# Six query and key pairs by seven half-size products, and partial sums kept in PSUM

## The chip, the cores and the metric

The kernel runs on one core of one Trainium2 chip. The metric is the device time of one execution in microseconds, and the median of several executions is given. TensorE is called PE in the profile (PEld is its loading of weights), VectorE DVE, ScalarE ACT, GpSimd POOL and the sync engine, which here only issues DMAs, SP. `L436` means line 436 of the kernel.

## The reference

The reference is a decoder trunk of two layers on 512 tokens of width 1024, in float32. The first layer mixes tokens by attention, the second by a recurrent block; a gated convolutional feed-forward follows each, and each of the four stages stands between two RMS norms.

```python
for layer in range(DEPTH):
    h = rms_norm(x, norm_mix_pre[layer])
    if layer % 2 == 0:
        h = dilated_attention_mixer(h, attn_w_qkv[j], attn_w_o[j], rel_bias)
    else:
        h = rglru_mixer(h, ...)
    x = x + rms_norm(h, norm_mix_post[layer])
    h = rms_norm(x, norm_ffn_pre[layer])
    h = conv_ffn(h, ffn_w_up[layer], ffn_conv_w[layer], ffn_conv_b[layer], ffn_w_down[layer])
    x = x + rms_norm(h, norm_ffn_post[layer])
```

The attention has three groups of eight heads of 128 columns: one looks at a window of 128 neighbouring tokens, the other two at every fourth and every sixteenth token. `attn_w_qkv` is 1024 x 9216, that is queries, keys and values of 1024 columns for each group. The heads of the three groups are weighed against each other by their softmax sums and projected by `attn_w_o`. In the feed-forward, `w_up` (1024 x 6144) gives a gate and a value half of 3072 columns; a convolution over three tokens runs along each column, the gate goes through GELU, and `w_down` leads back to 1024.

## The kernel before

**Precision.** A float32 operand is split into a high part, rounded to the matmul's input type (fp32r), and a low part, the rest. A product is three matmuls: high by high, high by low, low by high (`PASSES`, L432). The activations of a stage lie turned in `hT`, high and low, 128 features x 512 tokens for each of eight feature blocks.

**Weights.** All of them stream from HBM. `add` (L195) puts chunks of 1 MB or less into `plan`, in the order of use, and their pieces into `splits`. `load` (L317) brings a chunk into one of two raw buffers by a DMA from SP; a raw buffer is free again when all pieces of its chunk are split. A chunk of the kinds `first` and `sum` is made by `add_up` (L298) instead: DMAs from POOL add one block of the weights onto another, in one tile that all sums in a row share; the next one's DMA is issued only when the pieces of the one named by `behind` are marked finished. `pump` (L231) takes the next piece of `splits`, in order: ScalarE writes the high part (L253), and VectorE the low part (L265), which `low_parts` (L263) issues when the next piece is split, or when `take` (L351) asks for that piece; only then is the piece marked finished. At most eight split pieces, called units, are in stock (`W_UNITS`). A piece is split only some ticks after its load was issued (`landed`, L260), unless `take` needs it at once. `tick` (L370) is called after each block of matmuls: it lets the side work (softmax, normalization, token sums) take a step, and calls `pump` for one or two units.

**Products.** `feat_tiles` (L650) computes 128 output features for all 512 tokens: eight feature blocks x three passes = 24 matmuls of 512 columns into one PSUM bank. There are eight banks; each product takes the next one, and its result is read by ScalarE or VectorE whenever they come to it. In the attention, `qk_sink` (L1258) copies a query bank with a scale by ScalarE (L1155) and a key bank by VectorE (L1157), in an order of tokens that suits the head.

**Seven products for eight.** A 2 x 2 product of halves can be made from seven half-size products of sums, in Strassen's way (here in Winograd's form). The kernel does so in three places. The values of the attention go through `value_steps` (L1209): features are halved, and weight columns are halved, and the seven products are spread over the steps of the attention by `step` (L1510) and `VALUE_STEPS`. Two pairs of `w_up` chunks in each feed-forward go through `sevenths` (L841), between the plain blocks of the same pair; `WIDE_STEPS` = (1, 3, 1, 2) says how many of the seven products follow each of the four plain blocks. A product there is 24 matmuls of 256 columns into a bank of its own (`product`, L844); results are gathered in the SBUF tiles `c` and `y` by VectorE (L874 to L891), and a block of the output is written by `out` (L859). The first two thirds of `w_down` go through `down_unit` (L968). The sums over the token side, T1 to T4, are made once for a stage by `token_sums` (L584): VectorE adds (L609), ScalarE writes the high part (L611), VectorE the low part (L615), one half in each of eight ticks, in the order T3, T2, T4, T1.

**The attention's order.** For each of four pairs of local heads, l0 to l3: two chunks of weights (queries, keys), each followed by a `step` of the values; then the pair's heads are put on the list of side work. Then for each of four pairs of strided heads, s0 to s3: four chunks (queries and keys of both groups), each followed by a `step`. The first step at which T1 is used is the last of the first seven.

## Time and profile before

| | |
|---|---|
| three runs | 1383.99, 1385.39, 1394.42 us |
| median | 1385.39 us |
| the profiled execution | 1389.3 us, span 1387.5 us |
| PE busy | 1355.5 us (98%), 7109 matmuls |
| DVE busy | 1048.3 us (76%) |
| ACT busy | 679.5 us (49%) |
| POOL busy | 111.3 us (8%) |
| HBM read, written | 218.23 MB, 28.36 MB |
| mean granted clock of PE | 0.996 |

The page divides the span into 40 slices of equal length. PE is at 8 tenths or more in all of them but the last, VectorE between 3 and 9, and the 16 DMA engines between 1 and 9, most in the first quarter, which is the attention. Its projection by `attn_w_o` begins at 433 us; the first feed-forward's wide pairs lie between 541 and 615 us and the second's between 1062 and 1136.

A row of the groups of instructions has the line, the engine, the operation, what it writes and reads, its shape and its count, then the busy time and the mean duration of one, then the idle time of the engine before it and what ended that. The mean of a matmul is its whole length through the array; matmuls in a row start at shorter intervals than that, so the length of a block is read from the chain, not from that mean. In the order of time a row has the start, the length, the engine and the instruction, and in brackets how long its engine was idle before it.

### The profile page before, as it was taken

The page shows a single profiled execution, that of the slowest core. Times are in us where ns is not written, and L with a number is a line of the kernel's source. Part 1 is how long each engine was busy: PE and PEld are TensorE (multiplying, and loading weights), DVE is VectorE, ACT ScalarE, POOL GpSimd, SP SyncE. Part 2 cuts the span into 40 slices and gives each one's busy share as a digit, 9 for nine tenths or more (in the row PEclk, how much of TensorE's full clock was granted, in tenths as well). Part 3 has the DMA queues.
Part 4 walks back from the last instruction along what each step waited for, and adds up shares of the span by engine and source line. Part 5 has one row for each costly group of instructions (what it writes and reads, how often), then busy time and mean ns, then how long its engine had stood idle before and what let it go on. Part 6 is the DMA issues. An engine that isn't in the chain of part 4 may idle for free.

```text
span 1387.5 us, 18700 instructions
## 1 busy us (share of the span) xinstructions
PE 1355.5 (98%) x7109; PEld 1200.3 (87%) x7109; DVE 1048.3 (76%) x1838; ACT 679.5 (49%) x1137; POOL 111.3 (8%) x126
## 2 busy tenths in 40 slices
PE   8999999999999989999999999999999999999997
PEld 6888888888888889998888888888899998888886
DVE  7786574636767678897978789778878897958785
ACT  5434342414355563455545545579663455535452
POOL 1211012011000001000000020000001000000020
PEclk9999999999999999999999999999999999999999
DMA  8979679696648264565767793233153665758771
GB/s 256 241 219 276 161 181 262 199 217 180 222 154 305 85 187 103 158 167 127 193 183 193 200 269 126 92 122 121 61 156 99 167 167 128 187 161 213 206 203 61
DMA packets 184237, 243.11 MB, mean 175 GB/s; under 512 B 16632, under 2 KB 135936, under 8 KB 184146
## 3 DMA queue, kind: packets, MB, share of 16 engines
q1 hardware_dynamic: 151456, 184.82, 40.7%
q0 software_dynamic: 32688, 57.09, 21.4%
q8 instruction: 56, 0.92, 0.3%
q14 instruction: 35, 0.29, 0.1%
q10 hardware_dynamic: 2, 0.00, 0.0%
HBM read 218.23 MB, written 28.36 MB: 178 GB/s over the span
## 4 chain that ended last, share of the span: by engine, by line
PE 30%; DVE 25%; ACT 9%; DMA 4%; issue 3%; DVEq 0%; ACTq 0%; SPq 0%; POOLq 0%
PE ps L436 16%; DVE wlo L265 7%; PE vq L634 5%; PE acc L436 5%; DVE u L822 5%; PE vq L436 3%; ACT whi L253 2%; DMA sum<-in_ffn_w_down_dram 2%; DVE xb L1581 1%; DVE x L552 1%; ACT u L818 1%; DVE run L609 1%; DVE post L547 1%; DMA raw<-in_ffn_w_up_dram 1%; DVE u L834 1%
## 5 line engine op out<-in xcount | busy, mean ns | idle before, releaser
L436 PE MATMUL ps<-hT,whi 128*128 128x512 f32 (+1 forms) x2528 | 698.8, 362 | 2.1 <-DVE hT L500 1.5
L436 PEld LDWEIGHTS ps<-hT,whi 128*128 128x128 f32 x2528 | 460.1, 190 | 59.2 <-DVE hT L500 2.2
L436 PE MATMUL ps<-hT,wlo 128*128 128x512 f32 (+1 forms) x1264 | 456.6, 361 | 1.5 <-DVE wlo L265 1.5
L265 DVE TENSOR_TENSOR wlo<-raw,whi 128x1024 fp32r<-128x1024 f32 x233 | 280.0, 1217 | 24.5 <-ACT whi L253 24.2
L253 ACT ACTIVATE whi<-raw 128x1024 fp32r<-128x1024 f32 x233 | 239.0, 1051 | 119.8 <-DMA raw<-in_attn_w_qkv_dram 82.9
L436 PEld LDWEIGHTS ps<-hT,wlo 128*128 128x128 f32 x1264 | 240.3, 190 | 29.8 <-DVE wlo L265 1.9
L822 DVE SCALAR_TENSOR_TENSOR u<-ps,cols,u 128x511 f32<-128x511 f32 (+1 forms) x160 | 119.5, 747 | 71.2 <-ACT u L818 68.3
L253 ACT ACTIVATE whi<-sum 128x1024 fp32r<-128x1024 f32 x68 | 70.7, 1050 | 143.8 <-DMA sum<-in_ffn_w_down_dram 65.2
L634 PE MATMUL vq<-whi,A 128*128 128x512 f32 x448 | 137.8, 379 | 0.0
L265 DVE TENSOR_TENSOR wlo<-sum,whi 128x1024 fp32r<-128x1024 f32 x68 | 81.9, 1217 | 57.6 <-ACT whi L253 57.6
L436 PE MATMUL acc<-whi,alo 128*128 128x512 f32 x256 | 97.2, 380 | 1.7 <-DVE alo L185 1.6
L436 PE MATMUL acc<-whi,ahi 128*128 128x512 f32 x256 | 98.2, 383 | 0.0
L436 PE MATMUL acc<-wlo,ahi 128*128 128x512 f32 x256 | 97.2, 380 | 0.6 <-DVE wlo L265 0.6
L634 PEld LDWEIGHTS vq<-whi,A 128*128 128x128 f32 x448 | 84.7, 189 | 12.0
L634 PE MATMUL vq<-wlo,A 128*128 128x512 f32 x224 | 85.1, 380 | 2.1 <-DVE wlo L265 2.1
L832 ACT ACTIVATE u<-u 128x512 f32<-128x512 f32 x48 | 30.3, 632 | 110.4 <-DVE u L822 110.4
L818 ACT ACTIVATE u<-ps,cols 128x512 f32<-128x512 f32 x80 | 61.0, 763 | 4.6 <-PE ps L436 4.6
L634 PE MATMUL vq<-whi,T 128*128 128x512 f32 x192 | 59.7, 382 | 0.0
L436 PEld LDWEIGHTS acc<-whi,alo 128*128 128x128 f32 x256 | 48.4, 189 | 9.2 <-DVE alo L185 2.5
L436 PEld LDWEIGHTS acc<-wlo,ahi 128*128 128x128 f32 x256 | 48.4, 189 | 7.8 <-DVE wlo L265 1.4
L436 PEld LDWEIGHTS acc<-whi,ahi 128*128 128x128 f32 x256 | 48.4, 189 | 6.6 <-ACT ahi L184 0.2
L634 PEld LDWEIGHTS vq<-wlo,A 128*128 128x128 f32 x224 | 42.3, 189 | 8.8 <-DVE wlo L265 2.9
(247 smaller groups left out, 1782.3 us busy)
## 6 DMA issues: line engine op xcount, KB each, us to landing
raw<-in_ffn_w_up_dram SPq DMA_DIRECT2D x44, 1024.0 KB
raw<-in_attn_w_qkv_dram SPq DMA_DIRECT2D x25, 1024.0 KB
raw<-in_ffn_w_down_dram SPq DMA_DIRECT2D x16, 1024.0 KB
sum<-in_ffn_w_down_dram POOLq DMA_DIRECT2D x16, 1024.0 KB, 8.7
sum<-in_attn_w_qkv_dram POOLq DMA_DIRECT2D x24, 512.0 KB, 8.4
raw<-in_attn_w_qkv_dram SPq DMA_DIRECT2D x16, 512.0 KB
sum<-in_ffn_w_down_dram SPq DMA_DIRECT2D x8, 1024.0 KB
raw<-in_lru_w_in_dram SPq DMA_DIRECT2D x8, 1024.0 KB
```

The costliest lines, as they stand in the source:

```text
L253: nc.scalar.activation(hi, raw, AF.Copy)
L265: nc.vector.tensor_tensor(lo, raw, hi.bitcast(F32), op=ALU.subtract)
L436: mm(dst, l[a], r[b], start=start and n == 0, stop=stop and n == 2)
L547: nc.vector.tensor_tensor(in_two(u[i]), unwoven(banks[i]), in_two(gh[i]), op=ALU.mult)
L552: nc.vector.scalar_tensor_tensor(xh[i], u[i], y, xh[i], op0=ALU.mult, op1=ALU.add)
L609: nc.vector.tensor_tensor(r[h], a, b[:, k], op=ALU.add if sg > 0 else ALU.subtract)
L634: mm(banks[u], act(a)[:, 2 * j + k, u * P : (u + 1) * P], woven(W[b][:, k, :]), start=(j, k, n) == (0, 0, 0), stop=(j, k, n) == (1, 1, 2),)
L818: nc.scalar.activation(u, ps, AF.Identity, scale=cc[:, j : j + 1], bias=cc[:, 48 + j : 49 + j])
L822: nc.vector.scalar_tensor_tensor(u[:, d:], ps[:, : S - d], wc, u[:, d:], op0=ALU.mult, op1=ALU.add)
L832: nc.scalar.activation(u, u, AF.Gelu_apprx_tanh)
L834: nc.vector.tensor_tensor(gv[k], gv[k], u, op=ALU.mult)
L1581: nc.vector.scalar_tensor_tensor(u[:, d:], ps[:, : S - d], wc, u[:, d:], op0=ALU.mult, op1=ALU.add)
```

## The change

Three things change.

First, six of the eight pairs of query and key chunks (l1 to l3 of the local heads, s0 to s2 of the strided ones, in these the group with the fourfold stride only) are computed by seven half-size products. The two loaded chunks stay as they are, and `w_crossed` names the seven pieces: three of the four sums that the scheme needs are added up in the left chunk's upper half, one in the right chunk's, by VectorE in place, each after the low part of the piece before. Both raw buffers belong to the pair until its fifth and its seventh piece are split. `crossed` issues the seven products one after the other, with a `pump` or a `tick` after each, and then both value steps that stood after the two chunks.

Second, the partial sums of the seven products stay in PSUM, there and in `sevenths`: a product is accumulated onto the bank of an earlier one. The banks are called X, W and Z. What is wanted of a bank before the next product is added to it is copied out by ScalarE (`kept`), three times in seven products, and the outputs are made from a bank and a copy.

Third, for this the signs of the token sums T2 and T1 are turned round, which changes operations in `value_steps`; and `prenorm` applies its two factors in one operation of VectorE for each half, where one product of the factors was made first and the second half went to ScalarE.

```diff
+CROSSED = [("l", 1), ("l", 2), ("l", 3), ("s", 0), ("s", 1), ("s", 2)]
...
+        if kind == "left":
+            return [raw[:, 0:4], (raw[:, 0:4], partner[i], 0), (raw[:, 0:4], partner[i], 4), raw[:, 4:8], (raw[:, 0:4], i, 4)]
+        if kind == "right":
+            return [raw[:, 4:8], (raw[:, 0:4], i, 4)]
...
-            if i in raws and state["live"] < W_UNITS and (now or landed(i)):
+            i2 = partner.get(i, i) if j in (1, 2) else i
+            if i in raws and i2 in raws and state["live"] < W_UNITS and (now or landed(i) and landed(i2)):
...
                 raw = opened[i][j]
+                if isinstance(raw, tuple):
+                    raw, other, k0 = raw
+                    low_parts()
+                    nc.vector.tensor_tensor(raw, raw, raws[other][:, k0 : k0 + 4], op=ALU.add)
...
+    def w_crossed(w, a, b):
+
+        n, m = (w_cols(w, c0, kind, False) for c0, kind in ((a, "left"), (b, "right")))
+        partner[n] = m
+        for key in ((n, 0), (n, 1), (n, 2), (m, 0), (m, 1), (n, 3), (n, 4)):
+            split_next(*key)
...
-        nc.vector.tensor_tensor(q, y, q, op=ALU.mult)
-        nc.vector.tensor_scalar(xs[0], xs[0], q, None, op0=ALU.mult)
-        nc.scalar.activation(xs[1], xs[1], AF.Identity, scale=q)
+        for i in range(2):
+            nc.vector.tensor_scalar(xs[i], xs[i], y, q, op0=ALU.mult, op1=ALU.mult)
...
+    def product_into(bank, W, act, first):
+
+        for n in range(2):
+            for k in range(4):
+                for p, (a, b) in enumerate(PASSES):
+                    mm(
+                        bank[:, n * 256 : (n + 1) * 256],
+                        W[a][:, k, n * P : (n + 1) * P],
+                        woven(act(b)[:, k, :]),
+                        start=first and (n, k, p) == (0, 0, 0),
+                        stop=(k, p) == (3, 2),
+                        skip_group_check=True,
+                    )
+        done()
+
+    def kept(bank, scale=1.0):
+        t = gen(s="c")
+        nc.scalar.activation(t, bank, AF.Copy, scale=scale)
+        return t
...
+            W, X, Z = psum("W"), psum("X"), None
+            product_into(W, take(n + 5, 0), total_of(3), True)
+            w5 = kept(W, -1.0)
             yield
-            q = product((n + 4, 0), corner(hT, 0, 0))
-            nc.scalar.activation(c, q, AF.Copy)
-            tt(y, y, q, op=add)
+            product_into(X, take(n + 4, 0), corner(hT, 0, 0), True)
+            c = kept(X)
             yield
-            q = product((n + 4, 1), corner(hT, 1, 0))
-            out(0, 0, c, q, add)
+            Z = psum("Z")
+            product_into(Z, take(n + 4, 1), corner(hT, 1, 0), True)
+            out(0, 0, c, Z, ALU.add)
             yield
-            q = product((n + 5, 1), total_of(2))
-            tt(y, q, y, op=sub)
-            tt(c, q, c, op=sub)
+            product_into(X, take(n + 5, 1), total_of(2), False)
+            u = kept(X, -1.0)
             yield
-            q = product((n + 7, 0), total_of(4))
-            out(1, 0, y, q, sub)
+            product_into(W, take(n + 7, 0), total_of(4), False)
+            out(1, 0, u, W, ALU.subtract)
             yield
-            q = product((n + 7, 1), total_of(1))
-            out(1, 1, y, q, add)
-            tt(c, c, q, op=add)
+            product_into(X, take(n + 7, 1), total_of(1), False)
+            out(1, 1, w5, X, ALU.subtract)
             yield
-            q = product((n + 8, 0), corner(hT, 1, 1))
-            out(0, 1, q, c, sub)
+            product_into(X, take(n + 8, 0), corner(hT, 1, 1), False)
+            out(0, 1, X)
...
+            X, W = psum("X"), psum("W")
+            product_into(X, take(n, 0), corner(hT, 0, 0), True)
+            c = kept(X, SCALE)
+            pump(1)
+            product_into(W, take(n, 1), total_of(3), True)
+            w5 = kept(W, -1.0)
+            tick()
+            product_into(X, take(n, 2), total_of(2), False)
+            u = kept(X, -1.0)
+            pump(1)
+            product_into(W, take(m, 0), total_of(4), False)
+            out(1, 0, lambda d, v: tt(d, v(u), v(W), op=ALU.subtract))
+            tick()
+            product_into(X, take(m, 1), total_of(1), False)
+            out(1, 1, lambda d, v: tt(d, v(w5), v(X), op=ALU.subtract))
+            pump(1)
+            Z = psum("Z")
+            product_into(Z, take(n, 3), corner(hT, 1, 0), True)
+            out(0, 0, lambda d, v: stt(d, v(Z), SCALE, v(c), op0=ALU.mult, op1=ALU.add))
+            tick()
+            product_into(X, take(n, 4), corner(hT, 1, 1), False)
+            out(0, 1, lambda d, v: nc.scalar.activation(d, v(X), AF.Copy, scale=SCALE))
+            tick()
+            for at in steps:
+                step(*at)
...
-            for j in range(2):
+            if ("l", hp) in CROSSED:
+                crossed(q, k, False, [("l", hp, j) for j in range(2)])
+            for j in range(0 if ("l", hp) in CROSSED else 2):
                 feat_tiles(1, hT, lambda m, ps: sink(2 * j + m, ps), not (hp or j), paired=False)
                 step("l", hp, j)
...
-            for j in range(4):
+            if ("s", hp) in CROSSED:
+                crossed(qs, ks, True, [("s", hp, j) for j in range(2)])
+            for j in range(2 if ("s", hp) in CROSSED else 0, 4):
...
+        if ("l", hp) in CROSSED:
+            w_crossed(qkv, hp * 256, D + hp * 256)
         for j in range(2):
-            w_cols(qkv, j * D + hp * 256)
+            if ("l", hp) not in CROSSED:
+                w_cols(qkv, j * D + hp * 256)
             value_part("l", hp, j)
```

`out` writes the four blocks of the pair, each in two operations of 256 columns, in the token order that the heads want.

More of the change, by code (lines that the diff above doesn't have):

```diff
@@ L209, in split_next, with parts_of @@
         todo[i] += 1
-    def parts_of(kind, raw):
+    partner = {}
+    def parts_of(i, kind, raw):
         if kind == "feat":
@@ L590, in token_sums @@
             4: [((1, 0), -1)],
-            1: [((0, 1), 1), ((0, 0), -1)],
+            1: [((0, 0), 1), ((0, 1), -1)],
         }
@@ L648, in each, with less @@
             nc.vector.tensor_tensor(dst[u], a[u], b[u], op=op)
+    def less(dst, a, b):
+        for u in range(2):
+            nc.vector.scalar_tensor_tensor(dst[u], a[u], -1.0, b[u], op0=ALU.mult, op1=ALU.subtract)
     def feat_tiles(n, hT, sink, halves=False, between=None, at=None, paired=True):
@@ L842, in sevenths, with out @@
             outs = {}
-            def product(piece, act, *then):
-                W = take(*piece)
-                q = psum("vq")
-                for n in range(2):
-                    for k in range(4):
-                        mm3(
-                            q[:, n * 256 : (n + 1) * 256],
-                            [w[:, k, n * P : (n + 1) * P] for w in W],
-                            [woven(act(a)[:, k, :]) for a in range(2)],
-                            k == 0,
-                            k == 3,
-                        )
-                done()
-                return q
-            def out(p, s, a, q, op):
+            def out(p, s, a, q=None, op=None):
                 if p not in outs:
@@ L1158, in qk, with crossed, views, out @@
             return o
+        def crossed(q, k, permute, steps):
+            n, m = chunk(), chunk()
+            o = {0: [gen(s="qk") for _ in range(2)], 1: [gen(s="qk") for _ in range(2)]}
+            q.extend(o[0])
+            k.extend(o[1])
+            def views(f, t, h):
+                dst = o[f][h]
+                if permute and f:
+                    return dst.rearrange("p (m t a k) -> p t m a k", m=16, t=2, a=2)[:, t], "p (k m a) -> p m a k", dict(m=16, a=2)
+                if permute:
+                    return dst.rearrange("p (r t a u) -> p t r a u", r=4, t=2, a=2)[:, t], "p (u r a) -> p r a u", dict(r=4, a=2)
+                if f:
+                    return dst.rearrange("p (t l j k) -> p t l j k", t=2, l=2, j=4)[:, t], "p (k j l) -> p l j k", dict(l=2, j=4)
+                return dst.rearrange("p (t a b) -> p t a b", t=2, a=2)[:, t], "p (b a) -> p a b", dict(a=2)
+            def out(f, t, op):
+                for h in range(2):
+                    dst, how, sizes = views(f, t, h)
+                    op(dst, lambda x: x[:, h * 256 : (h + 1) * 256].rearrange(how, **sizes))
+            tt, stt = nc.vector.tensor_tensor, nc.vector.scalar_tensor_tensor
+            X, W = psum("X"), psum("W")
[23 more added lines that the diff above has]
+                step(*at)
         def first_values():
@@ L1229, in value_steps @@
             product(q, total_of(2))
-            each(y, q, y, ALU.subtract)
-            each(c, q, c, ALU.subtract)
+            each(y, q, y, ALU.add)
+            each(c, q, c, ALU.add)
             yield
@@ L1234, in value_steps @@
             product(q, corner(hT, 1, 1))
-            each(c, q, c, ALU.subtract)
+            each(c, q, c, ALU.add)
             yield
@@ L1239, in value_steps @@
             o = [gen(s="v") for _ in range(2)]
-            each(o, y, q, ALU.subtract)
+            less(o, y, q)
             out(1, 0, o)
@@ L1244, in value_steps @@
             product(q, total_of(1))
-            each(y, y, q, ALU.add)
-            each(c, c, q, ALU.subtract)
+            less(y, y, q)
+            each(c, c, q, ALU.add)
             out(1, 1, y)
```

30 lines of the change are left out of this document (17 added, 13 removed).

## The prediction

> **What bounds the kernel now.** I read the page's totals first, then the chain of waits cut to the feed-forwards, then the activations and the vector instructions in order of time around the same products, then busy time by stage, then the waits and the DMA issues.
>
> ```profile
> span 1387.5 us, 18700 instructions
> PE 1355.5 (98%) x7109; PEld 1200.3 (87%) x7109; DVE 1048.3 (76%) x1838; ACT 679.5 (49%) x1137; POOL 111.3 (8%) x126
> ```
>
> TensorE is busy for 98% of the span; whether it also runs at its floor the chain shows, here through a feed-forward's first wide pair (start, length, what):
>
> ```profile
> 541.45 2.68 PE vq L436 x24
> 544.12 5.18 PE ps L436 x24
> 549.31 8.04 PE vq L436 x72
> 557.34 5.18 PE ps L436 x24
> ...
> 570.39 5.36 PE vq L436 x48
> ...
> 588.79 8.04 PE vq L436 x72
> ```
>
> 24 matmuls of 512 columns take 5.18 us, 24 of 256 columns 2.68 us (vq is a half-size product), and nothing stands between them. So every microsecond that TensorE waits in this stage is a microsecond of the total, and less work for the other engines brings nothing here. The second thing to see is how late those engines are (start, length, then the instruction; the first three are ScalarE's copies of a second product, the others VectorE):
>
> ```profile
> 562.13 0.57 ACT L873 ACTIVATE c<-vq 128x512 f32<-128x512 f32 x1
> 598.09 0.58 ACT L873 ACTIVATE c<-vq 128x512 f32<-128x512 f32 x1
> 1083.22 0.58 ACT L873 ACTIVATE c<-vq 128x512 f32<-128x512 f32 x1
> ```
> ```profile
> 55.96 1.23 DVE L265 TENSOR_TENSOR wlo<-sum,whi 128x1024 fp32r<-128x1024 f32 x1 [4.75 <-ACT whi L253]
> ...
> 84.30 0.68 DVE L615 TENSOR_TENSOR T<-run,T 128x512 fp32r<-128x512 f32 x1
> ...
> 574.51 1.22 DVE L219 TENSOR_TENSOR sum<-sum 128x1024 f32<-128x1024 f32 x1 [2.43 <-DMA sum<-in_ffn_w_up_dram]
> ...
> 582.80 0.81 DVE L865 TENSOR_TENSOR w<-y,vq 128x256 f32<-128x256 f32 x2
> ```
>
> The second product of the first wide pair ended at 549.31+2.68 = 551.99; its copy came at 562.13, ten microseconds later. Today that costs nothing, since each product has a bank of its own. Busy time by stage, cut at the first matmul of the second, third and fourth pair of local heads (length, PE, PEld, DVE, ACT, POOL with counts, granted clock, DMA share, GB/s):
>
> ```profile
> 55.56:89.78 34.22, 34.22 (x160) 29.86 (x160) 31.54 (x68) 18.14 (x34) 5.04 (x6) 1.00 0.76 215
> 89.78:123.89 34.11, 34.11 (x161) 29.94 (x161) 27.31 (x60) 12.60 (x26) 8.26 (x10) 1.00 0.93 256
> 123.89:173.97 50.08, 47.91 (x241) 42.69 (x241) 23.03 (x53) 16.72 (x33) 3.23 (x3) 0.97 0.78 194
> ```
>
> In the first two VectorE is within a few microseconds of full.
>
> **Part 1, TensorE in the six pairs.** A pair of query and key chunks is four blocks of 24 wide matmuls, 4 x 5.18 = 20.72 us; it becomes seven half-size products, 7 x 2.68 = 18.76. That saves 1.96 us a pair, **-11.8 us** for six. No DMA is added; bytes and issues stay.
>
> **Part 2, VectorE and ScalarE in the six pairs.**
>
> ```profile
> L265 DVE TENSOR_TENSOR wlo<-raw,whi 128x1024 fp32r<-128x1024 f32 x233 | 280.0, 1217 | 24.5 <-ACT whi L253 24.2
> L253 ACT ACTIVATE whi<-raw 128x1024 fp32r<-128x1024 f32 x233 | 239.0, 1051 | 119.8 <-DMA raw<-in_attn_w_qkv_dram 82.9 <-DMA raw<-in_ffn_w_up_dram 18.0 <-DMA raw<-in_ffn_w_down_dram 12.8
> L865 DVE TENSOR_TENSOR w<-y,vq 128x256 f32<-128x256 f32 x16 | 7.0, 482 | 0.0
> L1157 DVE COPY qk<-ps 128x512 f32<-128x512 f32 x16 | 10.9, 684 | 10.6 <-PE ps L436 10.6
> ```
>
> Seven weight units instead of four: three more low parts, 3 x 1.22. Four sums in place, at the row of the only such sum there is today: 4 x 1.22. Outputs: six half-bank operations (6 x 0.48) for two copies (2 x 0.68). VectorE gets 3.66+4.88+1.5 = about 10 us more a pair; ScalarE three splits and about 1.4 us of copies. With it the second and third local pair hold 41 and 37 us of VectorE work beside 32 of TensorE: VectorE becomes the bound there. From the fourth pair on (23 of 50) there is room on average.
>
> **Part 3, where TensorE will wait.** The units are split in order, eight ahead. Eight units of 5.18 us were up to 41 us of cover; eight of 2.68 are 21.
>
> (a) *Bank shared in the wide pairs.* Order of banks: W, X, Z, X, W, X, X. The fourth product adds onto X, so it must wait until ScalarE has copied the second out of X, with one product between. In the first pair the third product ends at 549.31+5.36 = 554.67, the copy at 562.13+0.57 = 562.70: 8.0 us of wait. Nothing ahead of the copy in ScalarE's queue changes: it comes behind the splits of the token sums, which wait for VectorE:
>
> ```profile
> 560.65 0.64 ACT L611 ACTIVATE T<-run 128x512 fp32r<-128x512 f32 x1 [3.65 <-DVE run L609]
> ```
>
> The second layer's copy (1083.22) belongs to the same schedule, so twice 8.0 = **+16**.
>
> (b) *Seventh product onto the sixth.* Both in X, back to back; VectorE must have read the sixth first. In the trace that read ends at 583.61, the sixth product at 570.39+2.68 = 573.07: 10.5 us late. But the wait in (a) lets VectorE catch up, and it has 3.7 us less to do a pair (four 0.68 and two 0.48 operations go). Bounds 0.8 (the read alone) and 10.5; I take the read and one low part partly ahead of it, 1.5, four times: **+6**. In a second wide pair the copy (598.67) is 4.5 us behind its third product (594.15); with the lag gone, 0.5, twice: **+1**.
>
> (c) *The last token sum in the first crossed pair.* That pair's fifth product is the first to use this sum, whose low part VectorE finishes at 84.30+0.68 = 84.98 today, in a queue that has been working since 55.96. TensorE reaches the product after four others and two heads' scores:
>
> ```profile
> 101.90 1.68 PE L1307 MATMUL S<-qk,qk 128*128 128x128 f32 x8
> ```
>
> 55.56 + 4 x 2.68 + 2 x 1.68 = 69.6. VectorE gets four sums ahead of it (+4.9) and loses the idle wait in the row of 55.96 (-4.75); so 85 stands, and **+15**, bounds 8 (that wait gone and half the sums later) and 20 (the sums alone).
>
> (d) *Two sums in a row.* In crossed pairs l1 and s0 both value steps follow the seven products, and the weights of both are added up by DMA in one tile. The second DMA is issued only when the low parts of the first are told done; today the next chunk's split flushes them, now the next chunk is the one that waits, so it happens when TensorE takes the first one's second unit. All later splits stand behind it.
>
> ```profile
> 635.95 5.18 PE vq L634 x24
> ```
> ```profile
> sum<-in_attn_w_qkv_dram POOLq DMA_DIRECT2D x24, 512.0 KB, 8.4
> sum<-in_attn_w_qkv_dram POOLq DMA_DIRECT2D x6, 1024.0 KB, 9.6
> ```
>
> 9.6 us to land at l1, plus half a split (1.05/2 + 1.22/2 = 1.1), less the value product of 5.18 that runs meanwhile: 5.5; at s0 it is two transfers of 8.4 side by side, about the same. Twice: **+11**, bounds 6 (issued while the product before still runs) and 18 (transfers one after the other). Then no unit is in stock: the next low part comes behind two combines of the value product, 2 x 0.68 + 1.22 = 2.6, twice: **+5**.
>
> (e) *The pair after it (l2), on an empty stock.* A summed unit goes VectorE, ScalarE, VectorE, 1.22+1.05+1.22 = 3.5 us against 2.68, and two heads' scores come between. By work 37 against 32, so 5; by the order up to 10, since each burst now delays TensorE at once. I take **+6**, near the work.
>
> (f) *ScalarE's three copies in a crossed pair* stand behind splits that wait for loads, and the product two later waits for the copy.
>
> ```profile
> ACT whi L253 <- DMA raw<-in_attn_w_qkv_dram: 82.9, 12, 14.1
> ```
>
> 82.9/12 = 6.9 us a wait, less the product of 2.68 between: 4 where a load is that late. I take one in four of the last four pairs, **+4**, bounds 0 and 16.
>
> (g) *Waits that go.* TensorE's own stalls of today shrink when it comes later; the clearest is this one, and its price is the clock's too (the second row is a cut of 5 us around it, columns as above):
>
> ```profile
> 133.29 1.68 PE L1346 MATMUL O<-PT,v 128*128 128x128 f32 x8 [2.17 <-DMA PT<-ltd]
> ```
> ```profile
> 134.00:139.00 5.00, 5.00 (x23) 4.53 (x22) 1.40 (x7) 1.68 (x3) 0.00 (x0) 0.66 1.14 313
> ```
>
> 2.17 of waiting and 0.34 x 5 = 1.7 at the lower clock, and I allow as much again for smaller ones: **-8**, bounds 0 and -10.
>
> (h) *The clock.* By that row a gap of TensorE is followed by 1.7 us lost. The five waits above of 5 us or more (two in (a), one in (c), two in (d)) give five of them: **+8**, bounds 0 and 14. [...]
>
> [...]
>
> **Part 4, the small edits.** The value products' signs change operations for others of the same shape; a pre-norm loses one tiny operation and moves one of 512 columns from ScalarE to VectorE: 0, between -2 and +2. The copies that the wide pairs lose are off the path there: 0.
>
> **The sum.** -11.8 + 16 + 6 + 1 + 15 + 11 + 5 + 6 + 4 - 8 + 8 = +52. The profiled execution took 1389.3 us, so 1441; the median of the runs shown is 3.9 lower, so **1438 us**.
>
> **Rivals.** *The saving arrives (faster).* The copies are late only because nobody hurries them, and come within one product (2.68 us) once somebody waits; the token sum is made in time. Then the 11.8 stay, with a few microseconds of (g): 1370 us. For it: the engines have idle time overall (76% and 49%). Against it: both queues are served in order, and the operations ahead of the copy and of the sum are there whether anyone waits or not. The point at which it decides is a copy within 2.68 us of its product's end; the rows show 10. Chance 0.10.
>
> *Only the wide pairs wait (no change).* Attention keeps its saving, (c) to (f) hide behind units in stock: -11.8 + 23 - 8 = +3, 1389 us. For it: the stage has eight units of stock. Against it: VectorE's 31.54 of 34.22. Chance 0.10.
>
> *VectorE bounds every crossed pair (slower still).* The stock never fills again: (f) at 16, (e) at 10, (d) at 18, (b) at 5 a pair, which is 12 + 4 + 7 + 14 more: 1475 us. For it: 10 us of VectorE work added to each; against it: from the fourth pair on it has half the time free. Chance 0.12.
>
> That the products cost other than 2.68 is hardly open: the same shapes with the same activations run in the wide pairs today.
>
> **How the numbers follow.** The forecast has 0.68. A measurement here tells about 1% from no change, that is 1371.5 to 1399.2. Faster by over 1% is the first rival alone, 0.10; within 1% the second, 0.10; slower the rest, 0.80. With (b), (c), (d), (f), (h) at their low ends and (g) at -10 the sum is +23, 1408; the upper end of the range is the third rival, the lower end is the second, 1389. Outside stay the first rival and about as much again for the spread around both ends. The forecast's own range is 1408 to 1462: its upper end adds to 1438 the upper ends of (c), (d) and (f), 5 + 7 + 12.
>
> **What would show it.** (a): in both feed-forwards the fourth product of the first wide pair starts only after ScalarE's copy, some 8 us after the third ends, and TensorE's waits name that line. (b): short waits for VectorE before each seventh product. (c): an idle TensorE before the fifth product of l1, ended by the token sum's low part near 85 us. (d): a gap of 5 to 6 us before the second value step of l1 and s0, ended by a sum's DMA. (h): a lower granted clock after them. The attention's output projection begins today at 433.57:
>
> ```profile
> 433.57 2.59 PE acc L436 x12
> ```
>
> The prediction is wrong if it begins earlier, or if the wide pairs stay without gaps; wrong in size if TensorE waits in all six pairs alike.

## The result, and the profile after

The changed kernel takes 1485.5 us (median of 4 runs, 1482.5 to 1486.7) against 1384.7 for the kernel before: a ratio of 1.0714, 95% interval 1.0656 to 1.0772. It is slower, as forecast, but by 101 us where the prediction had 53, and above the range's upper end, the 1475 of the third rival. The profiled execution's span went from 1387.5 to 1480.7 us, +93.2.

The page's totals (busy time and share of the span by engine, instructions):

```profile
PE 1374.9 (93%) x7541; PEld 1229.5 (83%) x7541; DVE 1096.3 (74%) x1878; ACT 706.4 (48%) x1177; POOL 111.5 (8%) x126
```

TensorE is busy 19.4 us longer, though 11.8 us of matmuls went, and idle for 1480.7 - 1374.9 = 105.8 us where it was 32.0. So the 93.2 are: -11.8 for the smaller products, +31.2 for matmuls that ran longer, +73.8 of waiting. VectorE's share of the span fell, from 76 to 74%. Who TensorE waited for, in total (engine, line, waited for; us, times, longest):

```profile
PE X L670 <- ACT c L682: 30.6, 9, 8.1
PE X L670 <- DVE qk L1228: 23.0, 5, 7.3
PE vq L656 <- ACT whi L185: 12.2, 2, 8.1
PE X L670 <- DVE w L899: 6.2, 4, 1.6
...
PE X L670 <- DVE T L638: 3.9, 1, 3.9
PE W L670 <- ACT c L682: 2.4, 3, 0.8
```

L670 is the matmul of the half-size products, L682 ScalarE's `kept` copy out of a bank, L1228 VectorE's writing of one output block of the keys, read from bank X, which the seventh product adds onto; L185 a split made only when TensorE already needs it; L899 the feed-forward's outputs.

In the feed-forward's first wide pair (ScalarE, then TensorE, in order of time: start, length, instruction, idle time before and what ended it):

```profile
635.64 0.63 ACT L629 ACTIVATE T<-run 128x512 fp32r<-128x512 f32 x1 [3.65 <-DVE run L627]
636.18 1.04 ACT L265 ACTIVATE whi<-raw 128x1024 fp32r<-128x1024 f32 x1
637.13 0.58 ACT L682 ACTIVATE c<-X 128x512 f32<-128x512 f32 x1
```
```profile
637.76 0.80 PE L670 MATMUL X<-T,whi 128*128 128x256 f32 x2 [8.12 <-ACT c L682]
660.48 0.49 PE L670 MATMUL X<-hT,whi 128*128 128x256 f32 x2 [1.56 <-DVE w L899]
```

That is the queue of the kernel before, the same 3.65 us of waiting for VectorE in front of the token sum included, now with TensorE behind it. The second layer has the same 8.12.

The attention lost most. Busy time by stage, each from the first matmul of one crossed pair to that of the next, the last one to the output projection (columns as in the prediction; first the three local and three strided stages of after, then the last three of before, whose first three the prediction shows):

```profile
54.29:112.81 58.52, 39.90 (x232) 36.11 (x232) 36.81 (x78) 17.97 (x36) 6.72 (x10) 0.83 0.65 172
112.81:157.65 44.84, 36.37 (x233) 33.74 (x233) 31.64 (x61) 17.32 (x33) 3.93 (x5) 0.92 0.51 136
157.65:210.91 53.26, 46.76 (x313) 43.48 (x313) 36.35 (x68) 23.12 (x41) 6.36 (x6) 0.97 0.81 209
210.91:298.80 87.89, 77.86 (x446) 69.94 (x446) 52.47 (x107) 30.04 (x51) 8.00 (x8) 0.92 0.53 141
298.80:387.01 88.21, 76.96 (x449) 70.42 (x449) 56.51 (x107) 33.25 (x66) 13.94 (x14) 0.94 0.77 211
387.01:508.68 121.67, 110.38 (x632) 100.43 (x632) 78.69 (x193) 51.57 (x126) 7.79 (x13) 0.96 0.61 184
```
```profile
173.97:247.79 73.82, 73.82 (x374) 65.08 (x373) 43.60 (x94) 25.20 (x43) 12.65 (x13) 1.00 0.87 223
247.79:322.46 74.67, 74.67 (x377) 66.32 (x377) 42.18 (x91) 29.68 (x60) 8.47 (x9) 1.00 0.70 187
322.46:433.09 110.63, 108.39 (x560) 95.93 (x560) 73.44 (x187) 44.97 (x118) 9.09 (x14) 1.00 0.67 204
```

Stage by stage: +24.3, +10.7, +3.2, +14.1, +13.5, +11.0. The local pairs cost 38 us and the strided pairs as much, although VectorE is idle for 35 and 32 us of the first two strided stages. What TensorE waits for there, in the first local and the second strided stage:

```profile
68.32 0.80 PE L670 MATMUL X<-T,whi 128*128 128x256 f32 x2 [6.64 <-ACT c L682]
82.33 0.38 PE L670 MATMUL X<-T,whi 128*128 128x256 f32 x1 [3.86 <-DVE T L638]
104.78 0.80 PE L656 MATMUL vq<-whi,hT 128*128 128x512 f32 x1 [8.12 <-ACT whi L185]
...
317.99 0.49 PE L670 MATMUL X<-T,whi 128*128 128x256 f32 x2 [2.63 <-ACT c L682]
332.53 0.80 PE L670 MATMUL X<-hT,whi 128*128 128x256 f32 x2 [7.29 <-DVE qk L1228]
```

And why VectorE reads the bank so late in the strided stage, though it has idle time (VectorE, then ScalarE; L1348 is the first of eight score operations of one head, L1488, named as what ScalarE waited for, the end of its small steps, L1493 the first of ScalarE's exponentials, L265 a split, L277 its low part):

```profile
322.52 0.41 DVE L1348 CUSTOM_DVE_ANT_1 L<-S,toe 128x128 f32<-128x128 f32 x1
...
330.23 1.22 DVE L277 TENSOR_TENSOR wlo<-raw,whi 128x1024 fp32r<-128x1024 f32 x1 [3.16 <-ACT whi L265]
331.37 1.11 DVE L1228 TENSOR_TENSOR qk<-c,X 128x256 f32<-128x256 f32 x2
```
```profile
325.97 0.20 ACT L1493 ACTIVATE s<-s 128x4 f32<-128x4 f32 x1 [8.03 <-DVE s L1488]
...
329.16 1.99 ACT L265 ACTIVATE whi<-raw 128x1024 fp32r<-128x1024 f32 x2
```

One head's scores hand over to ScalarE, whose exponentials stand ahead of a split, whose low part stands ahead of the read. 322.5 to 332.5 is ten microseconds, of which VectorE idles in 3.16. The fifth product, on the same bank, had started its last matmul at 322.3, and only one half-size product (2.68) stood between it and the next one on that bank.

### The profile page after: what moved, and what is told of

Its sections match the earlier page's. It is cut to its first block, busy times and chain, and to the rows that moved or that the text cites. A ratio compares the mean times of both kernels' runs of the same rounds, so it can differ in the third digit from the quotient of the medians.

```text
span 1480.7 us, 19620 instructions
## 1 busy us (share of the span) xinstructions
PE 1374.9 (93%) x7541; PEld 1229.5 (83%) x7541; DVE 1096.3 (74%) x1878; ACT 706.4 (48%) x1177; POOL 111.5 (8%) x126
## 4 chain that ended last, share of the span: by engine, by line
PE 56%; DVE 18%; ACT 8%; issue 3%; DMA 2%; SPq 0%; DVEq 0%; POOL 0%; ACTq 0%
PE ps L455 29%; PE vq L656 13%; PE acc L455 7%; DVE wlo L277 4%; PE X L670 3%; ACT whi L265 2%; DVE u L868 2%; DVE run L627 1%; DVE xb L1665 1%; PE W L670 1%; PE O L1546 1%; DVE L L1348 1%; ACT u L864 1%; DVE raw L251 1%; ACT L L1455 1%
## 5 line engine op out<-in xcount | busy, mean ns | idle before, releaser
L455 PE MATMUL ps<-hT,whi 128*128 128x512 f32 (+1 forms) x2144 | 582.9, 359 | 0.8 <-DVE hT L518 0.6
L455 PEld LDWEIGHTS ps<-hT,whi 128*128 128x128 f32 x2144 | 387.8, 190 | 46.9 <-ACT whi L265 1.3
L455 PE MATMUL ps<-hT,wlo 128*128 128x512 f32 (+1 forms) x1072 | 383.5, 358 | 1.5 <-DVE wlo L277 1.5
L277 DVE TENSOR_TENSOR wlo<-raw,whi 128x1024 fp32r<-128x1024 f32 x251 | 302.6, 1219 | 52.8 <-ACT whi L265 52.8
L265 ACT ACTIVATE whi<-raw 128x1024 fp32r<-128x1024 f32 x251 | 258.2, 1051 | 135.2 <-DVE raw L251 85.8
L455 PEld LDWEIGHTS ps<-hT,wlo 128*128 128x128 f32 x1072 | 203.8, 190 | 24.6 <-DVE wlo L277 1.9
L265 ACT ACTIVATE whi<-sum 128x1024 fp32r<-128x1024 f32 x64 | 66.5, 1052 | 70.9 <-DMA sum<-in_ffn_w_down_dram 57.3
L670 PE MATMUL X<-T,whi 128*128 128x256 f32 x320 | 67.6, 315 | 34.4 <-ACT c L682 30.6
L670 PE MATMUL X<-hT,whi 128*128 128x256 f32 x320 | 62.3, 299 | 29.3 <-DVE qk L1228 23.0
L670 PEld LDWEIGHTS X<-T,whi 128*128 128x128 f32 x320 | 57.9, 223 | 37.2 <-ACT c L682 32.7
L277 DVE TENSOR_TENSOR wlo<-sum,whi 128x1024 fp32r<-128x1024 f32 x64 | 77.0, 1219 | 11.5 <-ACT whi L265 11.5
L670 PEld LDWEIGHTS X<-hT,whi 128*128 128x128 f32 x320 | 54.5, 211 | 32.2 <-DVE qk L1228 23.1
```

Of the source, the lines that this page charges most:

```text
L265: nc.scalar.activation(hi, raw, AF.Copy)
L277: nc.vector.tensor_tensor(lo, raw, hi.bitcast(F32), op=ALU.subtract)
L455: mm(dst, l[a], r[b], start=start and n == 0, stop=stop and n == 2)
L670: mm(bank[:, n * 256 : (n + 1) * 256], W[a][:, k, n * P : (n + 1) * P], woven(act(b)[:, k, :]), start=first and (n, k, p) == (0, 0, 0), st ...
```

## The experiments

Each run is given as its median over the kernel before measured beside it (1386.0, 1383.9 or 1384.5 us). The change stands at +101 (+91 to +107 by its interval, which is wide because one of the four runs before took 1394.4 us). By the bare medians, without the kernel before, what a run gives back against the change comes out up to 2 us smaller or 1 us larger.

**The two halves.** First the feed-forwards' part alone: `CROSSED = []`.

> The feed-forwards' part alone: no pair of queries and keys is crossed (an empty list), the partial sums in PSUM stay in the wide pairs. Theory A (each part costs what the trace of after shows in its own stage): the output projection of the attention begins where it did before, near 434 us; each feed-forward has one wait of about 8 us before the fourth product of its first wide pair, 1.6 us before the seventh product of its second, and a slower clock behind the first, 12.7 us in the first layer and 11.7 in the second: 1385 + 24 = 1409 us. Rival: the waits in the feed-forwards are carried over from the attention that ends late; then 1385 to 1390.

Measured 1403.9 us, +18; ratio 1.0125 (1.0106 to 1.0143). Its waits:

```profile
PE X L670 <- ACT c L682: 16.2, 2, 8.1
PE X L670 <- DVE w L899: 6.2, 4, 1.6
```

The waits are there to the tenth, without any crossed pair. The total is 5 us below expectation: the attention ends 6 us earlier than in the trace of before (the first matmul of its output projection starts at 427.3, not 433.3); the run of the small edits below takes that up.

Then the attention's part alone, with the seven products of the wide pairs in a bank each and VectorE combining them, as before:

```diff
-            product_into(X, take(n + 5, 1), total_of(2), False)
-            u = kept(X, -1.0)
+            q = product((n + 5, 1), total_of(2))
+            tt(y, q, y, op=add)
+            tt(c, q, c, op=add)
```

> The attention's part alone: six crossed pairs as in the change, the feed-forwards' seven products in a bank each, combined by VectorE as before. Theory A: the wide pairs have no gaps, the output projection begins near 509 us as in after: 1485 - 24 = 1461 us. Rival (carried over): the gaps in the feed-forwards stay in some part, 1470 to 1485.

Measured 1458.2, +72; ratio 1.0514 (1.0491 to 1.0538). No wide pair has a gap left, and the output projection begins at 511.9. The halves add up within the change's interval: 18 + 72, and 4.5 that the small edits give in both, make 94.5.

**The small edits**: no crossed pair, no partial sums; what is left of the change are the signs and the pre-norm; of the latter the change makes this:

```diff
-        nc.vector.tensor_tensor(q, y, q, op=ALU.mult)
-        nc.vector.tensor_scalar(xs[0], xs[0], q, None, op0=ALU.mult)
-        nc.scalar.activation(xs[1], xs[1], AF.Identity, scale=q)
+        for i in range(2):
+            nc.vector.tensor_scalar(xs[i], xs[i], y, q, op0=ALU.mult, op1=ALU.mult)
```

> The small edits alone: no pair is crossed, the feed-forwards combine by VectorE from a bank for each product; what is left of the change are the signs of two token sums with the operations that follow from them, and the pre-norm. Theory: 0, between -2 and +2 us, 1384 to 1388. Rival: they bring some of the 6 us by which the attention ended earlier in the run with the feed-forwards' part alone: 1379 to 1382.

Measured 1380.0 against 1384.5; ratio 0.9965 (0.9947 to 0.9984). A small gain, and the only kernel of these that beats the one before. The row of TensorE's waits before the transposes of normalized rows, of before and of this run, goes with it:

```profile
PE tr L490 <- DVE xs L481: 7.1, 5, 3.1
```
```profile
PE tr L508 <- DVE xs L500: 4.0, 3, 2.6
```

Its output projection begins at 429.1, which is 4 of the 6 us above. In this run's trace the clock also never falls before the end (mean granted clock 0.999), where it fell twice before (0.996). Whether the rest is the edits' or a DMA that landed better (the wait of 2.17 us for PT is 1.31 here) isn't told apart.

**The queue that blocks itself** (step (d)): the low part that a sum's DMA waits for is given to VectorE at once.

```diff
             i = total["next"]
+            if i < state["raw"] and total["open"] and plan[i][2] == 512 and any((x[0], x[1]) == after[i] for x in late):
+                low_parts()
             if i < state["raw"] and total["open"] and after[i] in finished:
                 add_up(i)
```

> After, with one edit: as soon as the next sum of weights by DMA waits only for the low part that was put off, that low part is given to VectorE at once, so the DMA is issued before TensorE needs it. Theory (step (d): the queue blocks itself): the two waits for ScalarE's split before the second value step, 8.1 us in the first crossed pair and 4.0 in the first strided one, go or shrink below 2, and with them the slow clock behind them (10.2 and 6.8 us at half clock): 1485 - 17 = 1468 us. Rival: the transfer would be late anyway, since VectorE's low part itself is late: the waits stay above 5 and 3 us, 1480 or more.

Measured 1454.9, +71, so 30 us less than the change; ratio 1.0514 (1.0497 to 1.0531). GpSimd's issue of the second sum in the first local pair, after and here:

```profile
92.46 1.34 POOL L323 DMA_DIRECT2D sum<-in_attn_w_qkv_dram  x1 [17.94 <-ACT qk L1235]
```
```profile
77.48 1.35 POOL L325 DMA_DIRECT2D sum<-in_attn_w_qkv_dram  x1 [3.77 <-DVE wlo L277]
```

(After, the bracket names ScalarE's output of the seventh product, which ended at 92.2 us; the low part that was put off had run from 90.63 to 91.81.) Issued 15 us earlier, it is no longer waited for: the row of the value products' waits for L185 is gone. The gain is larger than the two waits and their clock, because the stock of units is no longer empty after them: the waits for low parts in the second local pair (7.8 us) go too. But in that pair a new wait of 5.07 us for VectorE's read before the seventh product appears, which was 0.69.

**The shared bank of the seventh product**: a bank of its own, and one copy by ScalarE.

```diff
             product_into(X, take(m, 1), total_of(1), False)
+            x = kept(X, SCALE)
...
-            product_into(X, take(n, 4), corner(hT, 1, 1), False)
-            out(0, 1, lambda d, v: nc.scalar.activation(d, v(X), AF.Copy, scale=SCALE))
+            Y = psum("Y")
+            product_into(Y, take(n, 4), corner(hT, 1, 1), True)
+            out(0, 1, lambda d, v: stt(d, v(Y), SCALE, v(x), op0=ALU.mult, op1=ALU.add))
```

> After, with one edit in the crossed pairs: the seventh product gets a bank of its own, ScalarE copies the sum after the fifth, and VectorE adds the two in the output. VectorE and ScalarE have 0.6 and 0.0 us more a pair. Theory A (the bank that is added onto is what costs): the five waits of TensorE for VectorE's read (0.7, 3.4, 4.4, 7.3, 7.3 = 23 us) go, and the slower clock behind four of them (some 2 us each): 1485 - 31 = 1454 us. Theory B (VectorE is late because it has too much to do, and what waits for it only moves to the next place): at most 10 us, 1475 or more.

Measured 1469.8, +84; ratio 1.0600 (1.0580 to 1.0621): 17 us less than the change, between the two theories. The 23 us of waits are gone and part of them stands at the next place, the low parts of the value product behind the pair (8.3 us in three waits, the longest in the first strided stage):

```profile
240.60 0.80 PE L656 MATMUL vq<-wlo,T 128*128 128x512 f32 x1 [4.69 <-DVE wlo L277]
```

**The softmax moved behind the read**, in the strided pairs.

```diff
             out(1, 0, lambda d, v: tt(d, v(u), v(W), op=ALU.subtract))
-            tick()
+            sooner = steps[0][:2] in (("s", 0), ("s", 1), ("s", 2))
+            if not sooner:
+                tick()
             product_into(X, take(m, 1), total_of(1), False)
             out(1, 1, lambda d, v: tt(d, v(w5), v(X), op=ALU.subtract))
+            if sooner:
+                tick()
             pump(1)
```

> After, with one step moved in the three strided pairs: the next head's scores and softmax come after the fifth small product on the shared bank and after VectorE's read of it, not before. No bank, no operation more or less. Theory (the read is late because the softmax of one head, with ScalarE's exponentials and a split between, stands ahead of it in VectorE's queue): the waits before the seventh products, 4.4 + 7.3 + 7.3 us, fall below 2 each: 1485 - 16 = 1469 us, down to 1462 with the clock. Rival (VectorE is late with low parts anyway): the waits stay above 4 us, 1480 or more.

Measured 1481.0, +97; ratio 1.0685 (1.0661 to 1.0709): no gain beyond the measurement. Yet the waits that it aimed at are gone altogether in the strided pairs. The row of VectorE's read keeps only the local pairs' share, and others have grown:

```profile
PE X L670 <- ACT c L682: 35.3, 9, 8.1
PE vq L656 <- ACT whi L185: 16.6, 2, 8.6
...
PE X L670 <- DVE qk L1230: 4.2, 2, 3.5
```

The reason for the late read was right (here it starts 0.5 us after its product's last matmul starts, where it was 6 to 9.5 us behind), and the conclusion wrong: without one head's scores between them the fifth product waits longer for ScalarE's copy (in the second strided pair 4.42, was 2.63), and the value products wait for low parts (5.2 us, four times).

**No shared bank in the crossed pairs**: all seven products in banks of their own, combined by VectorE.

```diff
-            product_into(X, take(n, 2), total_of(2), False)
-            u = kept(X, -1.0)
+            r = product_of(take(n, 2), total_of(2))
+            tt(y, y, r, op=ALU.subtract)
+            stt(z, r, SCALE, c, op0=ALU.mult, op1=ALU.add)
```

> Crossed pairs without partial sums in PSUM: each of the seven products has a bank of its own in all six pairs, combined by VectorE (four full operations and two halves more, 3.7 us a pair; one copy fewer and two halves fewer for ScalarE), and the feed-forwards combine by VectorE as before. Against the run with the attention's part alone (1458): theory A (waits for shared banks): the waits for copies (15 us) and for reads before the seventh products (22 us) go; as the run with the seventh product's own bank gave back about half of such a wait later, 1458 - 25 = 1433 us. Theory B (VectorE's and ScalarE's work in order is late whatever the banks): the waits move to low parts, and 22 us more of VectorE work eat the rest: 1452 or more.

Measured 1449.1, +65; ratio 1.0473 (1.0454 to 1.0492): 7 us less than with the attention's part alone (+72), 3 us below what theory B allowed and 16 above theory A. The waits for copies and for reads of a shared bank are gone, and what stands in their place is mostly this:

```profile
PE vq L656 <- DVE wlo L277: 15.0, 5, 4.1
PE vq L656 <- ACT whi L185: 13.1, 2, 8.0
PE vq L670 <- DVE T L638: 11.1, 3, 5.1
```

The token sums, waited for with 3.9 us in the change, are waited for with 11.1, all in the first crossed pair, once no shared bank holds TensorE up before them. VectorE also has 20 us more to do than there (1127.2 us busy, 1107.7), and the run doesn't tell the price of that from the price of the lateness.

**Only the second and third strided pair**, with the same banks of their own: `CROSSED = [("s", 1), ("s", 2)]`.

> The same, with only the second and third strided pair crossed, where VectorE had half its time free before. Theory A: no bank is shared and VectorE has room, so the saving of 2 x 1.96 us arrives less a wait or two: 1386 - 3 = 1383, between 1379 and 1387 us. Theory B: the seven small products reach every late operation sooner, and the low parts' waits cost more than they save: 1390 to 1400 us.

Measured 1395.3, +11; ratio 1.0083 (1.0067 to 1.0100). This run has the small edits too, so against the run of these (1380.0, -4.5) the two pairs that save 3.9 us of matmuls cost about 16. In these two stages VectorE was idle for 44 and 34% of the time before. What grew most is the row of waits for low parts of the value products, 11.9 us (2.7 with the small edits alone), most of it right behind each pair:

```profile
285.54 0.48 PE L656 MATMUL vq<-wlo,hT 128*128 128x512 f32 x1 [4.50 <-DVE wlo L277]
359.13 0.80 PE L656 MATMUL vq<-wlo,T 128*128 128x512 f32 x1 [4.09 <-DVE wlo L277]
```

**VectorE's added work on weights**: the 24 sums in place left out.

```diff
                     low_parts()
-                    nc.vector.tensor_tensor(raw, raw, raws[other][:, k0 : k0 + 4], op=ALU.add)
```

> After without the 24 sums of weights in place by VectorE (left out, so the products of the six pairs are made with wrong weights): 24 x 1.22 = 29 us less for VectorE, and ScalarE's splits don't wait for them. Theory B (VectorE's added work decides): most of the attention's waits go, 1485 - 50 = 1435 us or less. Theory A: the waits for banks stay, since the softmax and the splits that stand ahead of the reads are there as before; what goes are the waits for low parts in the second and third local pair (3.9 + 7.8) with a slower clock: 1470 us, and the waits for VectorE's read before the seventh products keep two thirds of their 23 us.

Measured 1464.6, +79; ratio 1.0567 (1.0541 to 1.0592; two runs): 22 us less than the change, nearer theory A, but not by its way. The low parts in the second local pair, which were to go, stay (7.1 of 7.8 us); what falls are the waits for ScalarE's copies, 33.0 to 21.7 us, since the splits ahead of the copies no longer stand behind VectorE's sums, and the matmuls, busy for 9.6 us less. The waits for VectorE's read don't shrink; in the second and third strided pair they grow to 8.76 and 8.77, since TensorE comes sooner.

**The clock by itself**: useless matmuls in the waits.

```diff
+    def fill(n, hT):
+        q = psum("fill")
+        for m in range(24 * n):
+            mm(q[:, :256], hT[0][:, m % 4, 0:P], woven(hT[0][:, m % 4, 0:256]), start=True, stop=True)
...
+            if j == 2:
+                fill(3, hT)
             product_into(X, take(n + 5, 1), total_of(2), False)
```

> After, with matmuls of no use (24 of 256 columns to a block, 2.68 us, into a bank of their own that nobody reads) put where TensorE waits: three blocks before the fourth product of each feed-forward's first wide pair (a wait of 8.1 us), one before the fifth product's successor on the same bank (2.6) and two before the seventh product (7.3) in the second and third strided pair. It measures the clock by itself. Theory (a gap costs its length and then a stretch at half clock): the ends of the waits don't move, and the slow stretches behind them go: 2.8 and 1.7 us in the feed-forwards, 2.8 in each of the two pairs: 1485 - 10 = 1475 us, with the granted clock at 1.0 there. Rival: the slower products behind a gap have another cause (operands, banks): the time stays or rises by up to 5.

Measured 1480.7, +97; ratio 1.0701 (1.0676 to 1.0726). In the feed-forwards it did what the theory says. From the start of the third product to the end of the fourth (both layers; of after, then of this run):

```profile
626.55:642.80 16.25, 8.13 (x51) 7.94 (x50) 15.47 (x23) 8.05 (x12) 0.76 (x1) 0.69 0.79 159
1157.79:1173.00 15.21, 7.09 (x50) 6.90 (x49) 14.43 (x22) 7.95 (x11) 0.84 (x1) 0.78 0.80 162
```
```profile
630.50:644.23 13.73, 13.67 (x122) 13.48 (x121) 12.95 (x19) 7.24 (x11) 0.73 (x1) 1.00 0.78 141
1159.77:1173.52 13.75, 13.66 (x122) 13.47 (x121) 12.97 (x19) 7.24 (x11) 2.16 (x2) 1.00 0.87 152
```

2.5 and 1.5 us less, and both layers now equal: what differed between them was the clock alone. In the strided pairs, where one block stood before the fifth product and two before the seventh, it brought nothing: 3.72 and 3.78 us of the waits were left open, and the clock fell in them all the same: the seventh products behind them took 5.28 and 5.17 us where one that waits for nothing takes 2.68.

**All three at once**: the edits of the seventh product's bank, of the early DMA and of the feed-forwards together.

> Six crossed pairs with three steps undone at once: the feed-forwards combine by VectorE (alone: 1485 - 1458 = 27 us less), the sum's DMA is issued early (31 less), the seventh product has its own bank (16 less). Theory A (three separate costs): 1485 - 74 = 1412 us. Theory B (one lateness of VectorE that each of them meets in another place): the gains overlap, 1425 or more.

Measured 1423.3, +39; ratio 1.0263 (1.0240 to 1.0286). Alone they gave 29, 30 and 17, together 62 of these 76: mostly separate costs. The overlap of 14 (11.5 by the bare medians) is no larger than what the change's interval leaves open; the time lies between what the two theories gave.

And the same without the 24 sums, to see what is left:

> The run with three steps undone, and the 24 sums of weights in place left out as well (wrong weights for the six pairs). Theory A (what is left over the kernel before is VectorE's added work on weights): it falls by 15 to 20 us against that run, and stands within 10 us of 1386. Theory B (units of half the size give less cover, whatever VectorE adds): it falls by less than 8 us.

Measured 1407.8, +23; ratio 1.0150 (1.0126 to 1.0174): 15.5 us less, as theory A has it, but not within 10 us of the kernel before. Of the remaining 23 us no single cause is shown; its largest rows of waiting are ScalarE's copies (12.9 us, most of it in the local pairs), low parts of the value products (7.9), the token sum (4.6) and one wait of 4.5 for VectorE's regrouping of the local heads' softmax sums. That units of half the size give less cover is a reason for it that is argued, not tested by itself; it stays open.

## Why the prediction was right in direction and wrong in size

The direction and the reason hold: engines whose lateness cost nothing became late for TensorE. The terms against the trace, in us:

- Smaller products: -11.8, and it is -11.8; a half-size product that waits for nothing takes 2.68.
- **(a)**: +16, measured 16.2. The copy came out of the same queue at the same delay, and the feed-forwards' run shows it without the rest.
- **(b)** in the feed-forwards: +6, measured 6.2. The copy in the second wide pair, +1: no wait.
- **(b) in the crossed pairs: nothing in the sum, measured 23.0.** This is the step that failed first. Step (b) counts the wait for VectorE's read in the four wide pairs, where the sixth product stands right before the seventh. In the crossed pairs one product (Z, 2.68 us) stands between the two, and the prediction gives neither a price for the wait there nor a reason to leave it out. The "5 a pair" of the rival "VectorE bounds every crossed pair" doesn't hold it either: its 14 more are 4 x (5 - 1.5), the wide pairs again. The runs show 0.7, 3.4, 4.4, 7.3 and 7.3 in five of the six pairs, in the strided ones since one head's scores, exponentials, a split and its low part stand ahead of the read, and a bank of its own for the seventh product gave 17 us back.
- **(c)**: +15, measured 3.9, but behind a wait of 6.6 for ScalarE's copy in the same pair, which (f) did not have there. The token sum was done at 82.3, near the 85 forecast; one lateness is paid once, at whichever place TensorE meets it first. Without shared banks it was 11.1.
- **(d)** with the empty stock: +16, and 12.2 of waiting for L185. **(e)**: +6, measured 7.8 of low parts in the second local pair. The size of (e) came out by luck: the prediction took it from VectorE's work, 37 us beside 32, but without the 24 sums 7.1 of the 7.8 stay, and with the DMA issued early they go. The two are one cause, and its run gave back 30 us with the clock.
- **(f)**: +4, measured 16.8, its upper bound. I looked for loads that are late; what stands ahead of the copies is the softmax's exponentials and the splits behind VectorE's sums (without the sums the copies are waited for 11.3 us less).
- **(g)**: -8, and the waits elsewhere fell by 14.9 (32.0 before; after, 17.1 of the 105.8 lie outside the six stages above and the wide pairs). Part of it comes from the small edits, which **Part 4** put at 0 and which measured -4.5 (-7 to -2).
- **(h), the clock: +8, against 31.2 of longer matmuls**, about 27 of them the clock's; besides (b) this is the term that was off by most. I counted five gaps of 5 us or more at 1.7 each. In the trace the clock is at half speed in 15 stretches before the end, 85 us in all, nine of them after waits of 2 to 5 us. Eight stretches last 6.8 or 10.2 us rather than 3.4; in these the wait ahead of the stretch goes on inside it (0.4 to 5.0 us of idle time), in the seven of 3.4 us there is 0.6 at most. TensorE is idle for 25 of the 85 us, so it works 60 at half speed (its matmuls of 256 columns start every 0.213 us there, 0.112 elsewhere) and at a granted clock of 0.5 loses 30, of which the kernel before had 3; this is an estimate from the records of the clock, and what the other 4 to 5 of the 31.2 are isn't shown. Nor need the 31.2 all be lost time: in the strided pairs, where VectorE's read ends the wait of 7.3 us, time won in the matmuls ahead of it would only lengthen that wait. This is argued, not shown.

So two sizes were wrong: the waits of the crossed pairs (66 us in the six stages against 41 in (c) to (f)) and the clock (27 to 31 against 8). That (c) to (f) measured 40.7 together, beside the forecast's 41, is luck: (c) was 11 too high and (f) 13 too low. What the sum lacked is the 23.0 of (b) in the crossed pairs. Behind the first is one sentence of Part 2: "From the fourth pair on (23 of 50) there is room on average." It was true, and VectorE still has a third of its time free there after the change; but an average says nothing of a chain that goes VectorE, ScalarE, VectorE in order, ten microseconds long, when the product that covers it has shrunk from 5.18 to 2.68. The sentence on what would make it wrong in size came true: TensorE waits in all six pairs, with 6.5 to 18.6 us in each.

The rival that came nearest in time (1475) had only part of the reason: of the 55 us of work that the crossed pairs add to VectorE (1107.7 us busy with the attention's part alone, 1052.4 with the small edits alone), the 24 sums of weights (28 us) are worth 22 us alone and 15.5 beside the other edits; the low parts and outputs, which are the rest, were not taken away by themselves.

A bank for each product gave back 29 us in the feed-forwards, the whole of that half, and in the crossed pairs only a part: 17 us for one bank, 7 for all of them (with 20 us more for VectorE to do), where the late engine is met again at the next low part (15.0 us of waiting, five times, with all of them).

## What to carry to other kernels

Before a product is made smaller or its result kept in a bank that the next one adds onto, look for the longest chain of handovers between the two vector engines around it, and compare it with the work that stands between the two uses of the bank; an engine's free time on average is no cover. When a wait is removed by moving its cause, ask what the moved work was covering: here a read came 6 to 9 us sooner and the time hardly changed. And price the waits of one stage together, not one by one: one lateness is paid once, but a gap of two microseconds can be paid again in the clock (before, 2.17 us of waiting and then 3.41 us at a granted clock of 0.50).

## What the runs showed of the hardware that was not expected

In these traces the clock falls by a grid, not by the length of one gap. In the records of the granted clock of all 14, every stretch at half clock begins a whole number of 3.413 us steps after the trace's first one, and all but the cut-off last are 1 to 4 steps long (after: 7, 6 and 2 of one, two and three steps). What goes with a fall is how long TensorE was idle within one step of that grid. Of the steps at full clock, 107 held more than 2.0 us of idle time, and after each of them the clock was at half; after none with less than 1.8 it was; between the two it was after 4 of 14. In the traces of before and after alone these are 17 of 17, none of 791 (the most idle of them 1.66 us) and 2 of 2 (1.90 and 1.96). So a wait of 2.17 us inside one step was enough in the kernel before, and one of 3.15 us, which two steps shared, was not (stretches of one step each, of before, columns as in the rows by stage; PE's busy time is the first after the length, the granted clock the third from the end):

```profile
130.75:134.17 3.42, 1.25 (x10) 0.96 (x8) 0.00 (x0) 0.00 (x0) 0.00 (x0) 1.00 1.12 314
134.17:137.58 3.41, 3.41 (x14) 3.23 (x14) 0.01 (x1) 0.26 (x1) 0.00 (x0) 0.50 1.15 305
495.98:499.39 3.41, 1.92 (x18) 1.73 (x16) 3.27 (x11) 1.57 (x6) 0.00 (x0) 1.00 0.04 14
499.39:502.81 3.42, 1.76 (x16) 1.76 (x17) 2.53 (x9) 2.43 (x6) 0.00 (x0) 1.00 0.88 297
502.81:506.22 3.41, 3.41 (x33) 3.41 (x32) 3.41 (x5) 3.20 (x4) 1.32 (x1) 1.00 0.44 151
```

A step at half clock with more than 0.7 us of idle time was always followed by another one (after: 9 of 9). Counting only gaps of 5 us, as the prediction did, finds 6 of the 15 falls of after; the other nine came behind waits of 2.2 to 4.4 us.
